# Gated DeltaNet layer: the sample states are updated fifty places later, and two key tiles trade PSUM banks

## The chip, the cores and the metric

The kernel runs on one core of one Trainium2 chip. The metric is the time of one execution on the device, in microseconds (us). TensorE is called PE in the profile, VectorE DVE, ScalarE ACT, GpSimd POOL and SyncE SP.

## The reference, cut to what matters

One inference step of a two-layer trunk on a prompt (16 meta tokens and 1024 tokens) and on eight samples of eight tokens. Layer 0 is a gated DeltaNet with 16 value heads, 8 key heads and a 128x128 state per head; layer 1 is an RWKV-7 mixer. The change is in layer 0:

```
g = -jnp.exp(a_log) * jax.nn.softplus(a + dt_bias)
L = jnp.where(strict, jnp.einsum('nbhik,nbhjk->nbhij', kb, k) * decay, 0.0)
sol = lax.linalg.triangular_solve(L + eye, rhs, lower=True, unit_diagonal=True)
def step(S, inp):                       # per chunk
    v_new = u_c - einsum('bhck,bhkv->bhcv', w_c, S)
    o = einsum('bhck,bhkv->bhcv', qd_c, S) + einsum('bhij,bhjv->bhiv', a_c, v_new)
    S = S * jnp.exp(gl_c)[..., None, None] + einsum('bhck,bhcv->bhkv', kd_c, v_new)
# samples: one chunk of 8 tokens each, S0 = state_gdn; the new S is returned as s_gdn
```

k is L2-normalised, so each key tile needs the squares of its columns before L can be scaled.

## The kernel before

Layer 0 works through eight head pairs j = 0 to 7 (one key head, two value heads h = 0 and 1). The tokens lie in nine tiles of 128: tile 0 holds the 64 sample tokens and the first prompt tokens. Projections run on segments of three tiles (s = 0, 1, 2).

The order on all engines is written out by hand. `Gaps` is a list of places. At each place TensorE gets six matmuls of the running projection (128x384 products), and then everything that was put at that place is issued, sorted by the second number of `put` (a lower one first, ties in the order of the calls). Each engine works its own instructions strictly in that order and waits where an operand is missing. An engine may run ahead of TensorE when its operands allow it, or behind.

Head pair j has its base at place B = 24 + 72 j. Around it:

- `prep_plan` makes the matrix L of pair j. Per segment s: `open_e` loads decays into E, four later steps mask them on GpSimd (L735) and take exponentials on ScalarE; `squares` (L758) multiplies each key tile with itself on TensorE into a PSUM bank and takes the diagonal on VectorE (L766), `rates` (L769 to L773) makes reciprocals, `scaled` (L780) multiplies the bank into E, and `blocks` stores diagonal blocks. The places k of `squares` are B-1, B+4 and B+7 for the three segments; `rates` and the first two tiles of `scaled` follow at k+1, the third tile at k+2. `norms` follows at B+9.
- `invert` inverts the 32x32 diagonal blocks in 31 steps of two instructions (L699, L701) from B+15 to B+48. For pairs 1 to 6 they run on GpSimd, for pairs 0 and 7 on VectorE. At B+49 and B+50 ScalarE copies the transposed inverse (L829), then DMAs spread it, and `merge` joins the blocks from B+57 on.
- `sample_read_plan` loads the sample states of both heads (tiles Sb, three buffers, 256 KB each) at B+12, B+15, B+16 and B+22 and reads them on TensorE at B+20 and B+28.
- `recur_plan` runs the recurrence over the nine tiles from R0 = B + 60, that is 12 places before the next pair's base. Tile t has r0 = R0 + 8 t. At r0: `a` (K times state, TensorE); r0+1: `solve` (X, VectorE L1053); r0+3: `b` (X with the inverse, then w on ScalarE); r0+5: `d` (state update and outputs), `reads`, `tokens`; r0+6: `state` (L1086) and `total` (o, L1107). `a` of the next tile needs the PSUM banks "r" that `total` reads. The sample update `sample_write_plan` is put from here too: per head it loads the state (L963), makes masked copies of tile 0's w on GpSimd (`spread`, L969, four instructions), scales the state on GpSimd (L973, eight instructions), multiplies on TensorE and adds on VectorE (`add`, L982, two banks) and stores (L985). It uses w and ktok of tile 0.
- Weights come in halves: fetch on SP into wraw (two buffers), whi cast on ScalarE, wlo on GpSimd (L150), at places 12 k + 2 and 12 k + 6.
- The convolutions of q, k and v run on ScalarE and VectorE (three taps, L643; tanh; the product L650), the z gate is a tanh on ScalarE and a product on VectorE (L920), one place later.

PSUM tags: "d" (two banks, projections), "r" (two), "f" (two), "m" (one) and "u" (one).

Of the kernel before, what the change touches and what calls it, by code (L numbers as in the profile page):

```python
# [95 lines left out]
class Builder:  # L96
# [8 lines left out]
    def t(self, pool, shape, tag, bufs=1, dt=F32):  # L105
        self.uid += 1
        return pool.tile(shape, dt, name=f"{tag}_{self.uid}", tag=tag, bufs=bufs)
# [638 lines left out]
    def prep_plan(self, j, B, G, o, pace):  # L746

        nc, t, fp, col, L = self.nc, self.t, self.fp, self.col, self.line
        ltd = self.dram([4, 18, 32, 32], f"ltd{j}")
        G.E, c = {}, Ctx()  # L750
        p_ = {}

        def open_e(s):
            G.E[s] = t(fp, [128, 3, 2, 128], "E", 3)
            G.Eg[s] = self.decays(j, s, G.E[s])
            next(G.Eg[s])

        def squares(s):  # L758
            if s == 0:
                c.kq, c.rec, c.bp = t(fp, [128, 9], "kq", 2), t(fp, [128, 9], "rec", 2), t(fp, [128, 9, 2], "bp", 2)  # L760
            p = p_[s] = self.ps(*(("f", 2) if j and s == 2 else ("u", 1)), "sc")
            for tt in range(3):
                b = slice(128 * tt, 128 * tt + 128)
                self.mm(p[:, b], G.K[s][:, b], G.K[s][:, b])
            for tt in range(3):
                nc.vector.scalar_tensor_tensor(p[:, 384:512], p[:, 128 * tt:128 * tt + 128], 1.0, self.ident, op0=ALU.mult, op1=ALU.mult,  # L766
                                               accum_out=c.kq[:, 3 * s + tt:3 * s + tt + 1])

        def rates(s):  # L769
            q3 = slice(3 * s, 3 * s + 3)  # L770
            nc.vector.tensor_scalar(c.kq[:, q3], c.kq[:, q3], 4e-6, None, op0=ALU.add)
            nc.vector.reciprocal(c.rec[:, q3], c.kq[:, q3])
            nc.vector.tensor_tensor(c.bp[:, q3], col[:, q3, 0, 2 * j:2 * j + 2], c.rec[:, q3].unsqueeze(2).broadcast_to([128, 3, 2]),  # L773
                                    op=ALU.mult)

        def scaled(s, *tts):
            E = G.E[s]
            for tt in tts:
                for h in (0, 1):
                    nc.vector.scalar_tensor_tensor(E[:, tt, h], p_[s][:, 128 * tt:128 * tt + 128], c.bp[:, 3 * s + tt, h:h + 1], E[:, tt, h],  # L780
                                                   op0=ALU.mult, op1=ALU.mult)

        def blocks(s):
            E6 = G.E[s].rearrange("p t h k -> p (t h) k")
            for r in range(4):
                b = slice(32 * r, 32 * r + 32)
                nc.sync.dma_start(ltd[r, 6 * s:6 * s + 6].rearrange("c s i -> s c i"), E6[b, :, b])

        G.Eg = {}
        for s in range(3):  # L790
            L.put(B - 10 + 4 * s + o, lambda s=s: open_e(s), 3)
            for u in range(3):
                L.put(B - 6 + 4 * s + o + u, lambda s=s: next(G.Eg[s], None), 2.6)
            L.put(B - 3 + 4 * s + o, lambda s=s: next(G.Eg[s], None), 2.6)
            k = B + (-1, 4, 7)[s] if j else B - 2 + 4 * s + o
            L.put(k, lambda s=s: squares(s), 2)
            L.put(k + 1, lambda s=s: rates(s), 1.8)
            L.put(k + 1, lambda s=s: scaled(s, 0, 1), 2)
            L.put(k + 2, lambda s=s: scaled(s, 2), 2)
            L.put(k + 4, lambda s=s: blocks(s), 3)  # L800
# [84 lines left out]
        for s in range(3):  # L885
            m = merge(s)
# [69 lines left out]
    def sample_write_plan(self, j, G, h, r):  # L956
        nc, t, L = self.nc, self.t, self.line
        hv = 2 * j + h
        Sb, c = {}, Ctx()

        def load(g):
            Sb[g] = t(self.gp, [128, 4, 128], "Sb", 3)
            nc.sync.dma_start(Sb[g], self.i["state_gdn"][0, 4 * g:4 * g + 4, hv].rearrange("b k v -> k b v"))  # L963

        def spread(*bs):
            if bs[0] == 0:
                c.we = t(self.gp, [64, 4, 128], "wexp", 1)
            for b in bs:
                nc.gpsimd.tensor_scalar(c.we[:, b], G.w0[h][0:64], self.bmask4[:, b:b + 1], None, op0=ALU.mult)  # L969

        def scale(g, *us):
            for u in us:
                nc.gpsimd.tensor_scalar(Sb[g][:, u], Sb[g][:, u], self.eglb[:, hv, 4 * g + u:4 * g + u + 1], None, op0=ALU.mult)  # L973

        def add():
            pss = [self.ps("m" if j < 7 else "u", 1, "sw"), self.ps("f", 2, "sw")]
            for g, ps in enumerate(pss):
                q = slice(32 * g, 32 * g + 32)
                self.mm(ps, G.kt0[q, h], c.we[q].rearrange("p b k -> p (b k)"))
            for g, ps in enumerate(pss):  # L980
                x = Sb[g].rearrange("p b k -> p (b k)")
                nc.vector.tensor_tensor(x, x, ps, op=ALU.add)  # L982

        def store(g):
            nc.sync.dma_start(self.o["s_gdn"][0, 4 * g:4 * g + 4, hv].rearrange("b k v -> k b v"), Sb[g])  # L985
        at = (1, 5 if h else 2, 4 if h else 1, 4, 5, 7, 8, 11, 13) if j < 7 else (1, 2, 1, 3, 4, 5, 5, 7, 9)
        for u, f in zip(at, (lambda: load(0), lambda: load(1), lambda: spread(0, 1, 2, 3), lambda: scale(0, 0, 1), lambda: scale(0, 2, 3),
                             lambda: scale(1, 0, 1), lambda: scale(1, 2, 3), add, lambda: (store(0), store(1)))):
            L.put(r + u, f, 2.8)

    def recur_plan(self, j, R0, G, sp):

        nc, t, L, col = self.nc, self.t, self.line, self.col
        hs = (0, 1)
        hv = lambda h: 2 * j + h
        attn, ag, kts, st = {}, {}, {}, {}
# [22 lines left out]
        def tokens(tg):  # L1019
            s, tt = divmod(tg, 3)  # L1020
            p = self.ps("m", 1, "ktok")
            self.transpose(p[:, 0:128], G.K[s][:, 128 * tt:128 * tt + 128])
            kt = kts[tg] = t(self.gp, [128, 2, 128], "ktok", 4)
            for h in hs:
                self.act(kt[:, h], p[:, 0:128], AF.Identity, scale=col[:, tg, 3, hv(h):hv(h) + 1])
            if tg == 0:
                G.kt0 = kt
# [27 lines left out]
        def b(tg):  # L1055
            s, tt = divmod(tg, 3)
            c = st[tg]
            c.w = [t(self.gp, [128, 128], "w", 4) for h in hs]
            if tg == 0:
                G.w0 = c.w  # L1060
            for h in hs:
                self.mm(c.part(h, 1), G.TT[s][:, 2 * tt + h, :], c.X[h])
            if tg:
                for h in hs:
                    self.mm(c.part(h, 3), c.q, G.S[:, h])
            for h in hs:
                self.act(c.w[h], c.part(h, 1), AF.Identity, scale=G.nbp[:, tg, h:h + 1])
# [46 lines left out]

        G.os, G.ssq = {}, {}
        L.put(R0 - 3, lambda: tokens(0), 1.5)
        for tg in range(9):
            r0 = R0 + sp * tg
            for u, f, prio in zip(o_at, (a, solve, b, d, state, reads, total, powers), (1, 1.1, 1, 1, 1.1, 1.2, 1.2, 1.9)):
                L.put(r0 + u, lambda f=f, tg=tg: f(tg), prio)  # L1120
            if tg < 8:
                L.put(r0 + o_at[8], lambda tg=tg: tokens(tg + 1), 1.5)
        for h in hs:
            self.sample_write_plan(j, G, h, R0 + (5 if sp == 8 else 3) + 8 * h)
        for s in range(3):
            n0 = R0 + 3 * sp * (s + 1)
            L.steps(n0, self.gdn_norm(j, G, s), (1, 3, 4, 5, 6), 1.8)
# [1570 lines left out]
```

## Time and profile before

| | us |
|---|---|
| median of three runs | 2204.52 |
| lowest, highest | 2193.73, 2209.86 |
| the profiled execution | 2204.94 |
| its span, first to last instruction | 2203.2 |

One line of the time-ordered view gives the start and the duration of a group of instructions, the engine, the line of the kernel, the operation, the tiles written and read, shapes and count; in square brackets stands how long the engine sat idle before it and whom it waited for. A line of the list of waits gives the total, the number and the longest. A window row gives, per engine, the busy time and the number of instructions, then the granted TensorE clock as a share of full speed.

### The profile page before, as it was taken

What the parts mean: (1) busy time and instruction counts of PE and PEld (TensorE: products, weight loads), DVE (VectorE), ACT (ScalarE), POOL (GpSimd) and SP (SyncE); (2) the same over time, 40 slices, a digit from 0 to 9 for tenths busy, and PEclk for the clock granted to TensorE, in tenths of its full rate; (3) what the DMA queues carried; (4) which work ended last, traced back from release to release, by engine and by line L of the source; (5) the groups of instructions that cost most, each with busy time, mean ns of one, the idle gap of its engine ahead of it and who ended that gap; (6) DMA issues with size and microseconds to landing.
All of it is one profiled execution on the core that took longest, in us unless ns stands there. A gap on an engine that the chain in (4) does not pass through costs nothing.

```text
span 2203.2 us, 56211 instructions
## 1 busy us (share of the span) xinstructions
PE 2087.2 (95%) x20990; PEld 1964.7 (89%) x20990; DVE 1487.7 (68%) x3761; ACT 1246.2 (57%) x3622; POOL 1197.1 (54%) x1788
## 2 busy tenths in 40 slices
PE   8889999999999999988999999999998989999996
PEld 7888989989898989987899999999898988899886
DVE  6867576675757676595533584378875636899976
ACT  5536555655556555654543365575654536777763
POOL 2426758575666858532623163126967424777751
PEclk8999999999999999999999999999999999999998
DMA  3323242424324242433616315478787566776643
GB/s 117 86 74 110 72 115 65 125 78 108 97 74 117 75 110 69 126 84 97 195 58 168 90 55 159 160 233 244 204 241 199 147 183 183 198 195 180 177 133 97
DMA packets 510764, 291.68 MB, mean 132 GB/s; under 512 B 240777, under 2 KB 495866, under 8 KB 510490
## 3 DMA queue, kind: packets, MB, share of 16 engines
q1 hardware_dynamic: 510490, 288.08, 46.7%
q8 instruction: 166, 2.72, 0.5%
q14 instruction: 108, 0.88, 0.1%
HBM read 195.66 MB, written 92.30 MB: 131 GB/s over the span
## 4 chain that ended last, share of the span: by engine, by line
PE 63%; DVE 17%; DMA 7%; ACT 6%; issue 3%; POOL 2%; SPq 2%; DVEq 0%; POOLq 0%; ACTq 0%
PE d L136 14%; PE dv L136 7%; PE dz L136 7%; PE rA L136 6%; PE dk L136 4%; DVE cvy L643 3%; PE rA L140 2%; PE do L136 2%; PE zo L136 2%; DVE E L780 2%; PE xX L140 1%; DMA wraw<-in_gdn_w_out 1%; PE fG L136 1%; DVE invtmp L699 1%; DVE invT L701 1%
## 5 line engine op out<-in xcount | busy, mean ns | idle before, releaser
L150 POOL TENSOR_TENSOR wlo<-wraw,whi 128x512 fp32r<-128x512 f32 x174 | 230.7, 1326 | 250.6 <-ACT whi L146 226.4
L643 DVE SCALAR_TENSOR_TENSOR cvy<-raw,cw,cvy 128x408 f32<-128x408 f32 (+2 forms) x288 | 204.3, 709 | 20.2 <-ACT cvy L122 15.4
L701 POOL TENSOR_TENSOR invT<-invT,invtmp 72x31 f32<-72x31 f32 (+27 forms) x310 | 199.4, 643 | 24.3
L699 POOL TENSOR_TENSOR invtmp<-invA,invT 72x31 f32<-72x31 f32 (+27 forms) x310 | 183.7, 593 | 22.5 <-DMA invA<-rltd 4.5
L136 PE MATMUL d<-xc,whi 128*128 128x384 f32 (+1 forms) x640 | 175.5, 339 | 0.5 <-ACT ev L1455 0.5
L146 ACT CAST whi<-wraw 128x512 fp32r<-128x512 f32 x238 | 146.0, 615 | 33.7 <-DMA wraw<-in_rwkv_w_rkvz 13.2
L136 PE MATMUL dv<-xc,whi 128*128 128x384 f32 (+1 forms) x480 | 156.8, 350 | 0.0
L136 PE MATMUL dz<-xc,whi 128*128 128x384 f32 (+1 forms) x480 | 149.9, 337 | 0.0
L122 ACT ACTIVATE w<-rA,nbp 128x128 f32<-128x128 f32 x144 | 45.3, 364 | 154.1 <-PE rA L136 142.0
L136 PEld LDWEIGHTS d<-xc,whi 128*128 128x128 f32 x640 | 116.8, 190 | 2.6 <-ACT ev L1455 0.9
L136 PE MATMUL d<-xc,wlo 128*128 128x384 f32 (+1 forms) x320 | 104.3, 336 | 1.0 <-DVE wlo L150 1.0
L136 PE MATMUL dv<-xa,whi 128*128 128x384 f32 (+1 forms) x288 | 104.1, 361 | 0.0
L136 PE MATMUL dz<-xa,whi 128*128 128x384 f32 (+1 forms) x288 | 100.3, 348 | 0.8 <-DVE zg L920 0.8
L136 PE MATMUL d<-xa,whi 128*128 128x384 f32 (+1 forms) x336 | 95.4, 336 | 0.7 <-POOL xa L150 0.7
L136 PEld LDWEIGHTS dv<-xc,whi 128*128 128x128 f32 x480 | 94.3, 199 | 0.0
L1967 POOL TENSOR_SCALAR y<-y,mv,grs 128x64 f32<-128x64 f32 x132 | 83.8, 653 | 18.7 <-DVE grs L171 17.1
L167 POOL TENSOR_TENSOR ors<-ovar,cvals 128x6 f32<-128x6 f32 x24 | 34.1, 1421 | 110.0 <-DVE ovar L1136 102.1
L136 PEld LDWEIGHTS dz<-xc,whi 128*128 128x128 f32 x480 | 90.1, 191 | 0.2
L973 POOL TENSOR_SCALAR Sb<-Sb,eglb 128x128 f32<-128x128 f32 x128 | 82.8, 659 | 2.0 <-DVE cvy L643 1.1
L136 PE MATMUL d<-xh,whi 128*128 128x384 f32 (+1 forms) x256 | 82.6, 335 | 0.8 <-ACT xh L146 0.8
L136 PE MATMUL d<-xl,whi 128*128 128x384 f32 (+1 forms) x256 | 82.8, 336 | 0.3 <-DVE sal L1598 0.3
L136 PE MATMUL d<-xh,wlo 128*128 128x384 f32 (+1 forms) x256 | 82.3, 335 | 0.0
(565 smaller groups left out, 7351.3 us busy)
## 6 DMA issues: line engine op xcount, KB each, us to landing
wraw<-in_gdn_w_in SPq DMA_DIRECT2D x96, 256.0 KB
wraw<-in_rwkv_w_rkvz SPq DMA_DIRECT2D x74, 256.0 KB
Sb<-in_state_gdn SPq DMA_DIRECT2D x64, 256.0 KB
wraw<-in_rwkv_w_o SPq DMA_DIRECT2D x48, 256.0 KB
E<-drow SPq DMA_DIRECT2D x24, 384.0 KB
attn<-drow SPq DMA_DIRECT2D x24, 384.0 KB
wraw<-in_gdn_w_out SPq DMA_DIRECT2D x36, 256.0 KB
out_s_gdn<-Sb SPq DMA_DIRECT2D x32, 256.0 KB
```

Source lines behind the costliest of these rows:

```text
L122: return self.nc.scalar.activation(out, in_, func, bias=bias, scale=scale, **kw)
L136: self.nc.tensor.matmul(out, lhsT, rhs, start=start, stop=stop)
L140: self.nc.tensor.matmul(out, lhsT, rhs, start=start, stop=True, skip_group_check=True)
L146: nc.scalar.copy(hi, x)
L150: e.tensor_tensor(lo, x, hi.bitcast(F32), op=ALU.subtract)
L167: self.nc.gpsimd.tensor_tensor(y, x, half.broadcast_to(sh), op=ALU.pow)
L643: nc.vector.scalar_tensor_tensor(ys[s][:, 0:wd(s)], raws[s][:, k:k + wd(s)], cw[k], ys[s][:, 0:wd(s)], op0=ALU.mult, op1=ALU.add)
L699: v.tensor_tensor(tmp, A[:, j, j + 1:32].unsqueeze(2).broadcast_to([nb, n, m]), Tv[:, j, 0:m].unsqueeze(1).broadcast_to([nb, n, m]), op=AL ...
L701: v.tensor_tensor(Tv[:, j + 1:32, 0:m], Tv[:, j + 1:32, 0:m], tmp, op=ALU.subtract)
L780: nc.vector.scalar_tensor_tensor(E[:, tt, h], p_[s][:, 128 * tt:128 * tt + 128], c.bp[:, 3 * s + tt, h:h + 1], E[:, tt, h], op0=ALU.mult, ...
L973: nc.gpsimd.tensor_scalar(Sb[g][:, u], Sb[g][:, u], self.eglb[:, hv, 4 * g + u:4 * g + u + 1], None, op0=ALU.mult)
L1967: nc.gpsimd.tensor_scalar(y[:, q], y[:, q], mv[:, q, 0:1], P.rs[:, q:q + 1], op0=ALU.subtract, op1=ALU.mult)
```

## The change

Three things change, all in layer 0.

1. The sample update of pairs 0 to 6 moves. With P = B + 72, the next pair's base (R0 = P - 12): head 0 had its loads at P-6 and P-5, its mask products at P-6, its scalings at P-3, P-2, P and P+1, its adds at P+4 and its stores at P+6. It now has loads at P+29 and P+30, mask products at P+29, scalings at P+38 to P+41, adds at P+44, stores at P+46. Head 1 had loads at P+2 and P+6, mask products at P+5, scalings at P+5, P+6, P+8 and P+9, adds at P+12, stores at P+14; it now has loads at P+42 and P+47, mask products at P+45, scalings at P+46, P+47, P+49 and P+50, adds at P+52, stores at P+54. Head 0's first bank is "u" in place of "m". Pair 7's update stays where it was.
2. So that w and ktok of tile 0 live that long, they have buffers of their own ("w0" two, "kt0" one); the other tiles' "w" has two buffers in place of four and "ktok" three in place of four.
3. In `prep_plan` of pairs 1 to 7 the second segment's `squares` moves from B+4 to B+1 and into a bank of "f"; the third's, still at B+7, takes "u", in which the first's lies.

```diff
-            p = p_[s] = self.ps(*(("f", 2) if j and s == 2 else ("u", 1)), "sc")
+            p = p_[s] = self.ps(*(("f", 2) if j and s == 1 else ("u", 1)), "sc")
...
-            k = B + (-1, 4, 7)[s] if j else B - 2 + 4 * s + o
+            k = B + (-1, 1, 7)[s] if j else B - 2 + 4 * s + o
...
-            pss = [self.ps("m" if j < 7 else "u", 1, "sw"), self.ps("f", 2, "sw")]
+            pss = [self.ps("m" if h and j < 7 else "u", 1, "sw"), self.ps("f", 2, "sw")]
...
-        at = (1, 5 if h else 2, 4 if h else 1, 4, 5, 7, 8, 11, 13) if j < 7 else (1, 2, 1, 3, 4, 5, 5, 7, 9)
-        for u, f in zip(at, (lambda: load(0), lambda: load(1), lambda: spread(0, 1, 2, 3), lambda: scale(0, 0, 1), lambda: scale(0, 2, 3),
+        if j < 7:
+            r += 51 + 8 * h
+            L.put(r - (7 if h else 15), lambda: spread(0, 1, 2, 3), 2.8)
+            at = (-10, -5, -6, -5, -3, -2, 0, 2) if h else (-15, -14, -6, -5, -4, -3, 0, 2)
+        else:
+            L.put(r + 1, lambda: spread(0, 1, 2, 3), 2.8)
+            at = (1, 2, 3, 4, 5, 5, 7, 9)
+        for u, f in zip(at, (lambda: load(0), lambda: load(1), lambda: scale(0, 0, 1), lambda: scale(0, 2, 3),
                              lambda: scale(1, 0, 1), lambda: scale(1, 2, 3), add, lambda: (store(0), store(1)))):
             L.put(r + u, f, 2.8)
...
-            kt = kts[tg] = t(self.gp, [128, 2, 128], "ktok", 4)
+            kt = kts[tg] = t(self.gp, [128, 2, 128], *(("ktok", 3) if tg else ("kt0", 1)))
...
-            c.w = [t(self.gp, [128, 128], "w", 4) for h in hs]
+            c.w = [t(self.gp, [128, 128], "w" if tg else "w0", 2) for h in hs]
...
-            self.sample_write_plan(j, G, h, R0 + (5 if sp == 8 else 3) + 8 * h)
+            self.sample_write_plan(j, G, h, R0 + 5 if sp == 8 else R0 + 3 + 8 * h)
```

## The prediction, on record before the changed kernel was run

> **What bounds the kernel now.** I read the page first, then the waits of TensorE, then one head pair in the order of time on each engine, then the same stretches as windows.
>
> ```profile
> PE 2087.2 (95%) x20990; PEld 1964.7 (89%) x20990; DVE 1487.7 (68%) x3761; ACT 1246.2 (57%) x3622; POOL 1197.1 (54%) x1788
> PE 63%; DVE 17%; DMA 7%; ACT 6%; issue 3%; POOL 2%; SPq 2%; DVEq 0%; POOLq 0%; ACTq 0%
> PE rA L136 <- DVE o L1107: 24.4, 10, 3.1
> PE mktok L133 <- DVE attn L1011: 6.0, 7, 0.9
> ```
>
> TensorE sets the end, and VectorE holds 17% of the chain that ended last. One wait of TensorE is ten times the rest: a(t), which needs VectorE's total of the tile before. Seven of the ten are one stall that comes once in each head pair. Here it is between pairs 3 and 4. I call P the base place of the following pair, so that a(3) of the old pair is at P+12, b(3) at P+15, b(7) at P+47, d(7) at P+49 and b(8) at P+55.
>
> ```profile
> 563.69 0.60 PE L136 MATMUL rA<-X,TT 128*128 128x128 f32 x4
> ...
> 569.68 0.33 PE L133 MATMUL mktok<-ident,K 128*128 128x128 f32 x1 [0.86 <-DVE attn L1011]
> ...
> 575.56 1.19 PE L136 MATMUL rA<-S,K 128*128 128x128 f32 x4 [2.67 <-DVE o L1107]
> ...
> 584.18 0.61 PE L136 MATMUL rA<-X,TT 128*128 128x128 f32 x4
> ...
> 591.65 0.61 PE L136 MATMUL rA<-S,K 128*128 128x128 f32 x4
> ...
> 592.85 1.08 PE L136 MATMUL usr<-Sb,kqm 128*32 128x128 f32 x32
> ...
> 596.73 0.61 PE L136 MATMUL rA<-X,TT 128*128 128x128 f32 x4
> ```
>
> Three places of work take 8.62 us after the stall (575.56 to 584.18) and 5.08 us one tile later (591.65 to 596.73), though the later stretch holds 32 more matmuls. The windows say why: clock 0.50 after the stall, 1.00 later.
>
> ```profile
> core 0: us, PE busy (x) PEld busy (x) DVE busy (x) ACT busy (x) POOL busy (x), PEclk, DMA share, GB/s
> 575.50:582.00 6.50, 6.44 (x20) 4.64 (x21) 4.24 (x14) 3.24 (x13) 1.02 (x3) 0.50 0.48 132
> 604.40:637.90 33.50, 33.50 (x258) 33.13 (x257) 21.59 (x49) 17.48 (x56) 30.72 (x50) 1.00 0.18 51
> ```
>
> The second row is the stretch to which the change sends work: GpSimd (POOL) is busy 30.72 of 33.50 us there, in 50 instructions with a hand-over between each two.
>
> **The change part by part.** *Removed from P-11 to P+12.* VectorE is behind from 550.7 to 575.6, and these are its rows:
>
> ```profile
> 559.52 0.51 DVE L650 SCALAR_TENSOR_TENSOR K<-raw,cvy 128x336 f32<-128x336 f32 x1 [2.25 <-ACT raw L122]
> ...
> 561.18 0.66 DVE L982 TENSOR_TENSOR Sb<-Sb,msw 128x512 f32<-128x512 f32 x1
> 561.78 0.67 DVE L982 TENSOR_TENSOR Sb<-Sb,fsw 128x512 f32<-128x512 f32 x1
> ...
> 563.29 1.24 DVE L773 TENSOR_TENSOR bp<-gcol,rec 128x6 f32<-128x6 f32 x1
> ...
> 565.61 2.08 DVE L643 SCALAR_TENSOR_TENSOR cvy<-raw,cw,cvy 128x408 f32<-128x408 f32 x2
> ...
> 571.48 0.17 DVE L773 TENSOR_TENSOR bp<-gcol,rec 128x6 f32<-128x6 f32 x1
> ...
> 588.12 1.37 DVE L643 SCALAR_TENSOR_TENSOR cvy<-raw,cw,cvy 128x408 f32<-128x408 f32 x2 [1.02 <-ACT cvy L122]
> ```
>
> The two adds of head 0 go (1.26 us). The bp that took 1.24 beside GpSimd's eight scalings took 0.17 without them (1.07 saved), the two taps 2.08 against 1.37 (0.7). The second tile's norms, now at P+1, fill the 2.25 us in which VectorE waited for ScalarE's tanh; in exchange VectorE waits at P+1 for their six matmuls, which TensorE reaches behind d(1) at about 554.7 and ends 0.85 us later, 1.06 after VectorE is free at 554.49. So 24.9 - 1.26 - 1.07 - 0.7 - 2.25 + 1.06 = 20.7: the total that a(3) needs ends near 571.4. TensorE was there at 575.56 - 2.67 = 572.9; without the 0.86 and without head 0's four matmuls (1.06, next part) it is there at 571.0. The second key tile is ready at 552.3, before its matmuls are reached, so the PSUM bank and the earlier place cost TensorE nothing; without that cover it would wait for the silu. VectorE's total and X of tile 2 come some 0.4 us later than now and may hold a(2) and b(2) by so much. I take a(3) at 571.9, **3.7 us earlier**, with a stall of 0.5 in place of 2.67. The wait of 0.86 has no drop of the clock behind it, so neither should 0.5. Then a(3) to b(3) takes 5.08 less the sample reads (1.08) instead of 8.62: **4.6 us earlier**. In all 8.3, two adds on TensorE (2.1) counted. The same stall in the other pairs:
>
> ```profile
> 199.97 1.09 PE L136 MATMUL rA<-S,K 128*128 128x128 f32 x4 [2.67 <-DVE o L1107]
> ...
> 208.59 0.61 PE L136 MATMUL rA<-X,TT 128*128 128x128 f32 x4
> ...
> 449.65 1.20 PE L136 MATMUL rA<-S,K 128*128 128x128 f32 x4 [2.67 <-DVE o L1107]
> ...
> 459.66 0.60 PE L136 MATMUL rA<-X,TT 128*128 128x128 f32 x4
> ...
> 700.05 0.68 PE L136 MATMUL rA<-S,K 128*128 128x128 f32 x4 [2.67 <-DVE o L1107]
> ...
> 707.05 0.61 PE L136 MATMUL rA<-X,TT 128*128 128x128 f32 x4
> ...
> 947.53 1.12 PE L136 MATMUL rA<-S,K 128*128 128x128 f32 x4 [2.65 <-DVE o L1107]
> ```
>
> From a(3) to b(3) most take 8.6 us; the third takes 10.0 and the fifth 7.0, so their gains are 9.7 and 6.7. Bounds of the gain: 3.0 (only the adds and the two stretched groups, with the rest taken back by the later tanh) and 8.9.
>
> The Trainium skill, "TensorE: Matmul & The Clock Gate", section on HAM oscillation, warns only of idle gaps above some 3.4 us; by it a stall of 2.67 would keep the clock, and the gain would lose 3.5 of its 4.6. No such gap is needed here: 2.67 us were followed by a clock of 0.50, and the measurement decides.
>
> *Added from P+29 to P+54.* Head 0's mask products (P+29), scalings (P+38 to P+41) and adds (P+44), head 1's (P+45, P+46 to P+50, P+52). For pairs 1 to 6 GpSimd works off the triangular inverse there:
>
> ```profile
> 560.64 2.35 POOL L969 TENSOR_SCALAR wexp<-w,bmask 64x128 f32<-64x128 f32 x4 [1.20 <-PE fsw L136]
> 562.97 2.34 POOL L973 TENSOR_SCALAR Sb<-Sb,eglb 128x128 f32<-128x128 f32 x4
> ...
> 604.44 1.27 POOL L150 TENSOR_TENSOR wlo<-wraw,whi 128x512 fp32r<-128x512 f32 x1 [0.44 <-ACT whi L146]
> ...
> 630.70 0.53 POOL L701 TENSOR_TENSOR invT<-invT,invtmp 72x175 f32<-72x175 f32 x1
> ...
> 637.39 0.25 POOL L701 TENSOR_TENSOR invT<-invT,invtmp 72x31 f32<-72x31 f32 x1
> ...
> 642.31 1.30 POOL L150 TENSOR_TENSOR wlo<-wraw,whi 128x512 fp32r<-128x512 f32 x1 [2.89 <-ACT whi L146]
> ...
> 657.00 1.33 POOL L167 TENSOR_TENSOR ors<-ovar,cvals 128x6 f32<-128x6 f32 x1 [11.17 <-DVE ovar L1136]
> ```
>
> From 604.44 to 637.64 it has no idle time; its idle time comes after. Before the inverse's last step stand 4 + 8 + 4 + 4 new instructions: 2.35 + 4.68 + 2.35 + 2.34 = 11.7 us, and the step ends at 649.4 on the old clock. The queues behind it:
>
> ```profile
> 637.67 1.24 ACT L829 COPY invA<-invT 72x256 f32<-72x256 f32 x2
> ...
> 642.13 0.49 ACT L122 ACTIVATE zg<-dz 128x384 f32<-128x384 f32 x1
> ...
> 632.81 0.61 PE L136 MATMUL rA<-X,TT 128*128 128x128 f32 x4
> ...
> 643.89 0.61 PE L136 MATMUL rA<-X,TT 128*128 128x128 f32 x4
> ```
>
> ScalarE's copies of the inverse follow the last step at once (637.64 to 637.67), so there is no slack.
>
> First wait: head 0's second add needs the scalings of P+41, emitted behind the step that ended at 631.23; with 2.35 + 4.68 ahead they end at 638.3. The add stands in VectorE's queue ahead of X of tile 7, so b(7) comes at 638.3 + 0.7 + 0.6 = 639.6 instead of 632.81 + 1.06: TensorE stalls 5.7 us, and its slow clock afterwards runs while GpSimd is still working. Second wait: ScalarE's copies start at 649.4 and the tanh of the z tile, 4.95 us of queue behind them (637.67 to 642.62), ends at 654.4; VectorE's product (0.5) waits for it, head 1's adds stand behind that (1.3), then X (0.6): b(8) at 656.8 instead of 643.89, **12.9 us later**, both adds included. The loads of the inverse move with it and meet merges that are as late; so do the casts. SP's six DMAs per head go to a stretch where it waits for GpSimd anyway; only the fourth load still follows a store by one place. ktok with three buffers and w with two add no wait, since d(t) has read them before b(t+1) writes. Bounds of the loss: 2.1 (all of GpSimd's work hidden, four matmul pairs remain) and 17.
>
> The upper bound is from a stretched row:
>
> ```profile
> 567.28 1.87 POOL L973 TENSOR_SCALAR Sb<-Sb,eglb 128x128 f32<-128x128 f32 x2 [0.22 <-DMA Sb<-in_state_gdn]
> ```
>
> Two scalings took 1.87 beside VectorE's taps, 0.35 more each than 0.59: twelve of the new ones so are 4 us. I take 0.59, since VectorE itself waits from the first add on. The Trainium skill, "SBUF — State Buffer", section on the two sides, has GpSimd blocked for the whole of a VectorE instruction with two SBUF inputs, which the taps are; by it the stretched price holds wherever taps run beside it.
>
> *Sum.* Four pairs 12.9 - 8.3 = +4.6 each, the third +3.2, the fifth +6.2, the last (its inverse is on VectorE, GpSimd has room) 2.1 - 8.3 = -6.2: 18.4 + 3.2 + 6.2 - 6.2 = +22. The profiled execution took 2204.94 us for a span of 2203.2 and lies 0.4 us above the median of the three runs. 2204.94 + 22 = **2227 us**.
>
> **The rivals.** *GpSimd hides it:* 7 x 6.2 = 43 less, 2162 us. For it: 15 us of idle time follow the inverse (2.89 and 11.17 among them). Against it: the copies sit on the inverse without slack. This is the other side of zero, and it decides by whether the last step ends more than some 6 us late. *Only the first wait counts,* as the stretch after b(7) catches up while TensorE's clock is low: loss 5.7 + 2.1 = 7.8, six pairs at -0.5 in the mean and the last at -6.2: 2196 us. *The stretched scalings* of the bound: 6 x 4 more, 2251 us. *The early stall stays:* squares at P+1 push the K taps, tanh and total back, gain 3.0: 6 x 9.9 - 0.9 = +58.5, 2263 us. *The clock would have stayed up without the change too,* in the sense of the page's 3.4 us: gain 3.5 less in seven pairs, 2251 us; the row with 0.50 speaks against it.
>
> **How the numbers follow.** Forecast 0.50, with its own range 2207 to 2247 (2.3 us of loss and 1 of gain in six pairs either way). Hidden 0.18, first wait only 0.15, stretched 0.10, stall stays 0.05, clock 0.02. One per cent is 22 us, about what a measurement of this kernel can tell from no change. Slower by more: 0.25 of the forecast's 0.50 (it lies on that edge) and the last three, 0.42. Within: 0.25 and 0.15, 0.40. Faster: 0.18. The range 2168 to 2256 leaves out the hidden case, up to its near edge, and the stall that stays: 2 in 10 at most.
>
> **What would show it.** The wait of a(3) for o below 1 us in all seven pairs and clock 1.00 behind it; POOL's busy share near full from P+26 to past P+50; ScalarE's copies of the inverse waiting for POOL's last step; VectorE's Sb adds waiting for POOL's scalings; b(7) and b(8) waiting for X, with a slow clock behind b(7). I am wrong if POOL still shows idle time before the last step, or if a(3) still waits.

## The result, and the profile after

| | before | after |
|---|---|---|
| median, us | 2203.11 (six runs, 2193.73 to 2209.86) | 2234.47 (six runs, 2231.77 to 2239.79) |
| span of the profiled execution, us | 2203.2 | 2230.9 |
| mean granted clock | 0.970 | 0.969 |

The ratio is 1.015, 95% interval 1.0122 to 1.0177: **1.5% slower**. In the two spans the difference is 27.7 us, in the medians 31.4 us; what follows accounts for the spans.

First the busy times and the chain that ended last, then lines from the list of waits of the kernel after (total, number of times, longest):

```profile
PE 2092.3 (94%) x20990; PEld 1968.2 (88%) x20990; DVE 1479.1 (66%) x3761; ACT 1245.6 (56%) x3622; POOL 1184.1 (53%) x1788
PE 50%; DVE 14%; POOL 12%; ACT 9%; DMA 8%; issue 4%; SPq 2%; DVEq 0%; POOLq 0%; ACTq 0%
ACT cvy L122 <- POOL raw L628: 38.8, 20, 4.1
ACT invA L829 <- POOL invT L701: 28.5, 6, 4.8
PE rA L136 <- DVE o L1113: 25.1, 16, 3.1
PE msw L136 <- ACT ktok L122: 19.9, 6, 3.3
```

Every engine's busy time is within 1.2% of what it was. But GpSimd, 2% of the chain before, holds 12% of it now, though it is busy 53% of the time. Two of the waits come six times, once in each pair whose inverse runs on GpSimd: ScalarE's copies of the inverse wait for GpSimd's last step, and TensorE's sample matmuls into bank "m" wait for ScalarE's ktok, whose read frees that bank. The wait for o is as long in total as before and sits elsewhere, as TensorE's rows show, from b(3) of pair 2 to b(3) of pair 3:

```profile
456.79 0.68 PE L136 MATMUL rA<-S,K 128*128 128x128 f32 x4 [1.22 <-DVE o L1113]
461.00 0.61 PE L136 MATMUL rA<-X,TT 128*128 128x128 f32 x4
...
496.67 0.68 PE L136 MATMUL rA<-S,K 128*128 128x128 f32 x4 [2.11 <-DVE o L1113]
502.23 0.61 PE L136 MATMUL rA<-X,TT 128*128 128x128 f32 x4
...
516.08 0.75 PE L136 MATMUL rA<-X,TT 128*128 128x128 f32 x4 [1.10 <-DVE X L1059]
...
527.61 0.69 PE L136 MATMUL msw<-wexp,kt 32*128 32x512 f32 x1 [3.31 <-ACT ktok L122]
...
533.48 0.60 PE L136 MATMUL rA<-X,TT 128*128 128x128 f32 x4
...
586.51 0.68 PE L136 MATMUL rA<-S,K 128*128 128x128 f32 x4 [1.22 <-DVE o L1113]
590.73 0.61 PE L136 MATMUL rA<-X,TT 128*128 128x128 f32 x4
```

a(3), a(6), b(7), head 1's matmuls behind a(8), b(8), and the next a(3) and b(3). The stall at a(3) fell from 2.67 to 1.22 us; three new ones stand at a(6), in front of b(7) and in front of b(8). The windows behind a(3), a(6) and head 1's matmuls, and the stretch that the prediction showed at 30.72 of 33.50 us for GpSimd:

```profile
core 0: us, PE busy (x) PEld busy (x) DVE busy (x) ACT busy (x) POOL busy (x), PEclk, DMA share, GB/s
456.80:461.00 4.20, 4.20 (x27) 4.20 (x28) 4.05 (x15) 3.09 (x13) 1.79 (x4) 1.00 0.31 86
496.70:502.20 5.50, 5.50 (x25) 5.50 (x26) 4.12 (x9) 2.27 (x7) 5.19 (x9) 0.69 0.00 0
527.60:533.40 5.80, 5.79 (x22) 4.55 (x23) 2.27 (x5) 4.79 (x15) 4.24 (x6) 0.71 0.55 124
481.00:526.00 45.00, 40.09 (x281) 38.04 (x279) 23.24 (x53) 17.69 (x57) 42.66 (x71) 0.96 0.24 67
```

The low clock has changed places too: 1.00 behind a(3), where it was 0.50, and 0.69 and 0.71 behind two of the new stalls.

Cut at b(3) and b(8), the starts of these matmuls give a balance for every pair (us; the sum of the last two columns is the change of one period):

| pair | b(3) to b(8) before | after | b(8) to next b(3) before | after | loss | gain |
|---|---|---|---|---|---|---|
| first | 60.00 | 72.52 | 64.88 | 57.26 | 12.52 | 7.62 |
| second | 59.87 | 72.50 | 66.32 | 57.25 | 12.63 | 9.07 |
| third | 59.72 | 72.48 | 64.80 | 57.25 | 12.76 | 7.55 |
| fourth | 59.71 | 72.18 | 63.16 | 57.26 | 12.47 | 5.90 |
| fifth | 59.71 | 72.46 | 64.89 | 57.28 | 12.75 | 7.61 |
| sixth | 59.71 | 72.16 | 64.80 | 57.27 | 12.45 | 7.53 |
| last | 86.55 | 91.69 | | | 5.14 | |

The six periods give +30.3 us; the first b(3) comes 7.1 us earlier (201.47 for 208.59), the last pair ends 5.1 later, and 0.6 is won back after it: 27.7.

**How GpSimd's lateness reaches TensorE.** Its own rows, between b(6) and b(8):

```profile
487.83 2.35 POOL L969 TENSOR_SCALAR wexp<-w,bmask 64x128 f32<-64x128 f32 x4
...
492.92 0.18 POOL L628 COPY raw<-raw 128x3 f32<-128x3 f32 x1
...
513.86 1.18 POOL L973 TENSOR_SCALAR Sb<-Sb,eglb 128x128 f32<-128x128 f32 x2
...
525.49 0.25 POOL L701 TENSOR_TENSOR invT<-invT,invtmp 72x31 f32<-72x31 f32 x1
...
546.57 1.36 POOL L167 TENSOR_TENSOR ors<-ovar,cvals 128x6 f32<-128x6 f32 x1 [12.73 <-DVE ovar L1142]
```

and those of ScalarE and VectorE that wait for them:

```profile
493.13 0.62 ACT L122 ACTIVATE cvy<-raw,cw 128x384 f32<-128x384 f32 x1 [4.06 <-POOL raw L628]
...
525.77 1.17 ACT L829 COPY invA<-invT 72x256 f32<-72x256 f32 x2 [4.74 <-POOL invT L701]
526.84 0.63 ACT L122 ACTIVATE ktok<-mktok,gcol 128x128 f32<-128x128 f32 x2
...
493.78 2.03 DVE L643 SCALAR_TENSOR_TENSOR cvy<-raw,cw,cvy 128x384 f32<-128x384 f32 x2 [3.30 <-ACT cvy L122]
...
515.08 0.69 DVE L982 TENSOR_TENSOR Sb<-Sb,fsw 128x512 f32<-128x512 f32 x1 [2.27 <-POOL Sb L973]
...
530.63 0.55 DVE L920 SCALAR_TENSOR_TENSOR zg<-zg,dz 128x384 f32<-128x384 f32 x1 [8.81 <-ACT zg L122]
```

Three chains can be read from them. Head 0's mask products (487.83, 2.35 us) delay a copy of 0.18 us (L628) by which the convolution gets its carried columns; ScalarE's first tap waits 4.06 for it (1.42 before), VectorE's taps 3.30 for ScalarE, o stands behind the taps, and a(6) waits 2.11. The last scaling of head 0 ends at 515.04; the add, X and b(7) follow. The inverse's last step ends at 525.74; the copies start at 525.77, ktok behind them at 526.84, and the sample matmuls at 527.61. And 12.73 us of idle time lie on GpSimd just after all that.

### The profile page after: what moved, and what is told of

The parts are those of the page before. It is cut to its first block, busy times and chain, and to the rows that moved or that the text cites. A ratio compares the mean times of both kernels' runs of the same rounds, so it can differ in the third digit from the quotient of the medians.

```text
span 2230.9 us, 56268 instructions
## 1 busy us (share of the span) xinstructions
PE 2092.3 (94%) x20990; PEld 1968.2 (88%) x20990; DVE 1479.1 (66%) x3761; ACT 1245.6 (56%) x3622; POOL 1184.1 (53%) x1788
## 4 chain that ended last, share of the span: by engine, by line
PE 50%; DVE 14%; POOL 12%; ACT 9%; DMA 8%; issue 4%; SPq 2%; DVEq 0%; POOLq 0%; ACTq 0%
PE d L136 13%; PE dz L136 6%; PE dk L136 4%; PE rA L136 4%; POOL invT L701 3%; POOL invtmp L699 3%; DVE cvy L643 2%; PE do L136 2%; PE rA L140 2%; PE zo L136 2%; POOL wlo L150 2%; POOL Sb L973 2%; PE dv L136 1%; POOL wexp L969 1%; PE xX L140 1%
## 5 line engine op out<-in xcount | busy, mean ns | idle before, releaser
L643 DVE SCALAR_TENSOR_TENSOR cvy<-raw,cw,cvy 128x408 f32<-128x408 f32 (+2 forms) x288 | 198.2, 688 | 40.0 <-ACT cvy L122 35.0
L136 PE MATMUL dz<-xc,whi 128*128 128x384 f32 (+1 forms) x480 | 157.8, 355 | 0.0
L136 PE MATMUL dv<-xc,whi 128*128 128x384 f32 (+1 forms) x480 | 150.7, 337 | 0.0
L136 PE MATMUL dz<-xa,whi 128*128 128x384 f32 (+1 forms) x288 | 107.1, 372 | 0.8 <-DVE zg L920 0.8
L136 PEld LDWEIGHTS dz<-xc,whi 128*128 128x128 f32 x480 | 97.2, 205 | 0.2
L136 PEld LDWEIGHTS dv<-xc,whi 128*128 128x128 f32 x480 | 89.7, 190 | 0.0
L150 DVE TENSOR_TENSOR wlo<-wraw,whi 128x512 fp32r<-128x512 f32 x64 | 49.5, 774 | 52.1 <-ACT whi L146 40.6
```

The source lines that it names most:

```text
L136: self.nc.tensor.matmul(out, lhsT, rhs, start=start, stop=stop)
L150: e.tensor_tensor(lo, x, hi.bitcast(F32), op=ALU.subtract)
L643: nc.vector.scalar_tensor_tensor(ys[s][:, 0:wd(s)], raws[s][:, k:k + wd(s)], cw[k], ys[s][:, 0:wd(s)], op0=ALU.mult, op1=ALU.add)
```

## The experiments

All are compared with the kernel before, on the same chip and in the same rounds; its median was 2197.14 us in the rounds of the first four and 2205.37 in those of the last four.

**1. The norms alone.** The kernel before with only the third part of the change:

```diff
-            p = p_[s] = self.ps(*(("f", 2) if j and s == 2 else ("u", 1)), "sc")
+            p = p_[s] = self.ps(*(("f", 2) if j and s == 1 else ("u", 1)), "sc")
...
-            k = B + (-1, 4, 7)[s] if j else B - 2 + 4 * s + o
+            k = B + (-1, 1, 7)[s] if j else B - 2 + 4 * s + o
```

> The kernel before with the third part of the change alone: the second segment's squares at P+1 in a bank of f, the third's in u. Theory (GpSimd has no room at P+29 to P+50, and that costs 12.8 us a pair against an early gain of 8): this part does no harm; VectorE's wait of 2.25 us at P+4 goes, 1.1 us of waiting at P+1 comes, so a(3) waits 1 to 2 us and 2172 to 2198 us come out. Rival (the norms' new place and bank cause the loss, by holding up the taps of K): 2210 us or more, with a(2) or a(3) waiting longer than before.

Measured: 2182.35 us, ratio **0.9923** (0.9894 to 0.9952). The wait of a(3) is short here although no sample update has moved, and a new wait, seven times 1.44 us, stands in front of head 0's second sample bank:

```profile
550.29 1.12 PE L136 MATMUL fsw<-wexp,ktok 32*128 32x512 f32 x2 [1.44 <-DVE E L780]
...
563.58 0.68 PE L136 MATMUL rA<-S,K 128*128 128x128 f32 x4 [0.85 <-DVE o L1107]
...
569.05 0.61 PE L136 MATMUL rA<-X,TT 128*128 128x128 f32 x4
```

From a(3) to b(3) it takes 5.47 us for 8.62 before, head 1's sample matmuls included in both; b(3) to b(8) stays at 59.7 in four of the six pairs and is 60.6 in the other two. The stall of a(3) is short because TensorE comes late, held up by the new wait: from b(8) to a(3) it takes 56.9 us in the mean of six pairs, for 56.2 before. What is won here lies behind a(3), where the clock is 1.00 in the window from 563.6 to 569.0. So a part of the change that is a gain was bound together with one that costs more.

**2. The move alone.** The kernel after, with those two lines put back.

> The changed kernel with the norms back at their old place and bank: the sample update moved, alone. Theory: GpSimd's queue is as in the changed kernel, so the stalls at a(6), b(7) and msw stay: 2225 to 2245 us. Rival (the norms cause the loss): 2160 to 2195 us, without these stalls.

Measured: 2248.1 us, ratio **1.0225** (1.0159 to 1.029), a little above the expected range. b(3) to b(8) takes 71.64 us, nearly as long as in the full change, and a(3) still waits:

```profile
PE rA L136 <- DVE o L1113: 37.5, 16, 3.2
PE msw L136 <- ACT ktok L122: 13.2, 6, 3.3
...
453.88 0.68 PE L136 MATMUL rA<-S,K 128*128 128x128 f32 x4 [2.92 <-DVE o L1113]
...
583.98 0.68 PE L136 MATMUL rA<-S,K 128*128 128x128 f32 x4 [2.93 <-DVE o L1113]
```

Taking two adds and eight scalings out of the early stretch does not shorten the stall. It does bring a(3) forward: from b(8) to a(3) it takes 54.2 us in the mean of six pairs, for 56.2 before. TensorE is there sooner too, 51.3 us behind b(8) in place of 53.6, so the stall, which is the difference of the two, hides what VectorE has gained. And a(3) to b(3) takes 4.22 us in five of the seven pairs in spite of the stall. From b(8) to b(3) the move alone wins 5.9 us a pair of the 7.6 that the full change wins. VectorE still waits for the tanh in front of the product of K; with the norms moved as well, in the kernel after, it does not:

```profile
439.91 0.51 DVE L650 SCALAR_TENSOR_TENSOR K<-raw,cvy 128x336 f32<-128x336 f32 x1 [1.97 <-ACT raw L122]
...
446.27 0.51 DVE L650 SCALAR_TENSOR_TENSOR K<-raw,cvy 128x336 f32<-128x336 f32 x1
```

The first row is from this experiment, the second from the kernel after.

**3. The added work on ScalarE.** The kernel after, with the mask products and scalings of pairs 0 to 6 at the same places on ScalarE:

```diff
+                if j < 7:
+                    self.act(c.we[:, b], G.w0[h][0:64], AF.Identity, scale=self.bmask4[:, b:b + 1])
+                    continue
...
+                if j < 7:
+                    self.act(Sb[g][:, u], Sb[g][:, u], AF.Identity, scale=self.eglb[:, hv, 4 * g + u:4 * g + u + 1])
+                    continue
```

> The changed kernel, with the mask products and scalings of pairs 0 to 6 on ScalarE in place of GpSimd, at the same places. Theory: GpSimd's queue is 14 us a pair shorter, ScalarE's copies of the inverse wait no longer, 9 us a pair more on ScalarE (24 x 0.37) fit beside its 17.5 of 33.5 us; the loss falls from 12.8 to between 2 and 5 us a pair: 2160 to 2190 us. Rival (the late adds themselves, their banks, or the smaller buffers of w and ktok cost the time, whatever engine scales): 2225 us or more.

Measured: 2191.45 us, ratio **0.9956** (0.9928 to 0.9983), just above the expected range. b(3) to b(8) falls from 72.48 to 65.08 us, the stall at a(6) and the one for ktok are gone, and b(8) waits for X:

```profile
511.67 0.64 PE L136 MATMUL rA<-X,TT 128*128 128x128 f32 x3 [2.73 <-DVE X L1065]
```

**4. The added work left out.** The kernel after, with one mask product in place of four and no scalings in pairs 0 to 6:

```diff
+            if j < 7:
+                nc.gpsimd.tensor_scalar(c.we, G.w0[h][0:64].unsqueeze(1).broadcast_to([64, 4, 128]), self.bmask4[:, 0:1], None, op0=ALU.mult)
+                return
...
-            for u in us:
+            for u in us if j == 7 else ():
```

> The changed kernel without the scalings of the sample state in pairs 0 to 6, and with one mask product of 64x512 in place of four: this part of the computation is left out, loads, adds and stores stay. GpSimd has 2.6 us a pair in place of 14. Theory: the stalls at a(6), b(7) and msw go almost wholly, 2155 to 2180 us. Rival (adds, banks or buffers): 2225 us or more.

Measured: 2192.0 us, ratio **0.9955** (0.9932 to 0.9978); slower than expected. b(3) to b(8) still takes 64.55 us, 4.8 more than before, and b(8) waits 1.48 us:

```profile
504.07 0.56 DVE L920 SCALAR_TENSOR_TENSOR zg<-zg,dz 128x384 f32<-128x384 f32 x1 [6.28 <-ACT zg L122]
504.54 0.68 DVE L985 TENSOR_TENSOR Sb<-Sb,msw 128x512 f32<-128x512 f32 x1
...
506.14 0.75 PE L136 MATMUL rA<-X,TT 128*128 128x128 f32 x4 [1.48 <-DVE X L1062]
```

So of the 12.76 us that this pair loses in the full change, 7.9 go with GpSimd's added work and 4.8 stay: 2.1 for four matmul pairs, 1.48 for this stall, 0.46 for a short one at a(6), and 0.8 of small changes. (The new buffers of w and ktok were not tested by themselves; what they cost is within these 4.8.) Head 1's adds stand in VectorE's queue between the gate's product, which waits for ScalarE anyway, and X. On top of the norms the move wins 5.1 us between b(8) and b(3) (62.4 in experiment 1 in the mean of six, 57.3 after) and loses these 4.8: even with GpSimd's work for nothing it would be worth about nothing. What also makes the whole slower than expected is the last pair, whose stretch from b(3) to b(8) takes 96.2 us here, for 86.6 before.

**5. GpSimd's time alone.** The kernel before, its sample update where it was, and 24 useless GpSimd instructions per pair at the places to which the change sends work:

```diff
+        if j < 7:
+            def more(n):
+                d = t(self.gp, [128, 104], "more", 1)
+                for _ in range(n):
+                    nc.gpsimd.tensor_scalar(d, self.ident[:, 0:104], self.eglb[:, hv, 0:1], None, op0=ALU.mult)
+            P = r + (7 if h == 0 else -1)
+            for u, n in ((45, 4), (46, 2), (47, 2), (49, 2), (50, 2)) if h else ((29, 4), (38, 2), (39, 2), (40, 2), (41, 2)):
+                L.put(P + u, lambda n=n: more(n), 2.8)
```

> The kernel before, sample update untouched, with 24 useless GpSimd instructions of 128x104 in pairs 0 to 6, at the places to which the change moves the mask products and scalings. They write a tile that nobody reads. Theory (GpSimd has no room there): the inverse's last step comes some 9 us later, ScalarE's copies of it wait 4 us or more, a(6) waits 2 us, and the time rises by 5 to 9 us in six pairs: 2225 to 2255 us. Rival (what costs time is VectorE's late adds, which wait for the scalings and hold up X; GpSimd alone is hidden): within 8 us of the kernel before.

Measured: 2279.22 us, ratio **1.0342** (1.0309 to 1.0375), more than expected:

```profile
ACT invA L829 <- POOL invT L701: 48.8, 6, 9.2
PE rA L136 <- DVE X L1061: 46.3, 10, 7.6
ACT cvy L122 <- POOL raw L628: 36.7, 13, 4.2
...
516.21 0.68 PE L136 MATMUL rA<-S,K 128*128 128x128 f32 x4 [2.21 <-DVE o L1115]
...
551.25 1.22 PE L136 MATMUL rA<-X,TT 128*128 128x128 f32 x4 [6.89 <-DVE X L1061]
```

The same waits come back without one DMA, matmul or add being moved: a(6) behind the copy of L628, the copies of the inverse behind the last step. b(3) to b(8) takes 70.81 us, 11.1 more than before, and b(8) to b(3) 2.1 more (66.9 for 64.8 in the mean of six): 13.2 in each of six pairs are 79, and the spans differ by 73.3 (2276.5 and 2203.2). That GpSimd's lateness alone slows the kernel is shown. The 11.1 us are more than the 7.9 that went in experiment 4, since the two costs of the change do not add up: GpSimd's work alone costs 11.1 (here), the rest alone 4.8 (experiment 4), both together 12.6. That fits two paths to b(8) of which the later sets its start.

**6. What the early stall hangs on.** The kernel before, its update where it was, with the mask products cut to one and the scalings left out as in experiment 4.

> The kernel before without the scalings of the sample state in pairs 0 to 6 and with one mask product in place of four (this part of the computation is left out); adds and norms stay where they were. Theory (GpSimd's scalings stretch VectorE's instructions with two SBUF inputs from P to P+9, by 1.8 us a pair): bp takes 0.17 and the two taps 1.4 us, a(3) waits about 1 us in place of 2.67, and with a clock that then stays up 2165 to 2185 us come out. Rival (these rows were long for another reason): a(3) still waits over 2.3 us, 2195 to 2205 us.

Measured: 2200.35 us, ratio **0.9988** (0.9967 to 1.0009): no difference. VectorE's taps do get shorter, and a(3) waits as long as ever:

```profile
556.30 0.97 DVE L773 TENSOR_TENSOR bp<-gcol,rec 128x6 f32<-128x6 f32 x1
...
558.34 1.31 DVE L643 SCALAR_TENSOR_TENSOR cvy<-raw,cw,cvy 128x408 f32<-128x408 f32 x2
...
567.82 1.19 PE L136 MATMUL rA<-S,K 128*128 128x128 f32 x4 [2.94 <-DVE o L1110]
```

The taps took 2.08 us before and take 1.31; bp took 1.24 and still takes 0.97; and further on nbp (L805), 0.21 before, takes 1.01. b(8) to b(3) is 0.5 us shorter in the mean of six pairs (64.27 for 64.81), b(8) to a(3) 0.8 (55.5 for 56.2). Of the 1.77 us that the prediction put down to these two groups, less than half was there to be won.

**7. The norms, with the new wait mended.** Experiment 1, and head 0's second sample bank from "u", since "f" now holds the second segment's squares at that time:

```diff
-            pss = [self.ps("m" if j < 7 else "u", 1, "sw"), self.ps("f", 2, "sw")]
+            pss = [self.ps("m" if j < 7 else "u", 1, "sw"), self.ps(*(("f", 2) if h or j == 7 else ("u", 1)), "sw")]
```

> The norms alone, and head 0's second add bank is u in place of f (pairs 0 to 6). With the norms alone msw's partner fsw waited 1.44 us in each of seven pairs for scaled(1), which holds an f bank at P+4. Theory: that wait goes, what TensorE does next comes as much earlier unless VectorE is late: 2168 to 2180 us against 2182 for the norms alone. Rival (VectorE is the bound there and a(3) waits longer instead): 2180 to 2185 us, with a(3)'s wait grown by about 1.4 us.

Measured: 2172.71 us, ratio **0.9862** (0.983 to 0.9893), with experiment 8 the fastest version found, ahead of both kernels. The wait for E is gone; part of it comes back at a(3), which TensorE now reaches sooner. From b(8) to a(3) it takes 54.8 us in the mean of six pairs, for 56.2 before, so here the norms do bring a(3) forward:

```profile
562.78 0.68 PE L136 MATMUL rA<-S,K 128*128 128x128 f32 x4 [1.57 <-DVE o L1107]
...
568.26 0.61 PE L136 MATMUL rA<-X,TT 128*128 128x128 f32 x4
```

**8. The same, with mask products and scalings on ScalarE** (the edit of experiment 3 on top of 7).

> As the run with the norms and the bank u, and the mask products and scalings of pairs 0 to 6 on ScalarE at their early places. Theory (GpSimd's share of the early stretch slows VectorE, and ScalarE has room): a(3)'s wait goes wholly, 2160 to 2178 us. Rival (ScalarE is full from P-3 to P+9: exponentials, casts, tanh): tanh and w come later, 2185 us or more.

Measured: 2174.39 us, ratio **0.9864** (0.9825 to 0.9903), the same as 7. Where the update stands early, the engine that scales doesn't matter, which agrees with experiment 6. The wait of a(3), expected to go wholly, stays at 1.53 us. Putting the added work into GpSimd's 12.73 idle us was not tried.

## Why the prediction was right, point by point

**The balance** was forecast as 8.3 gained and 12.9 lost in a pair, +4.6; measured are 7.6 and 12.6, +5.0. The two odd pairs came out as read from their old stalls: +3.56 for the forecast +3.2, +6.57 for +6.2. In the whole: a first gain of 7.1 for 8.3, six periods of +30.3 for +27.8, the last pair +5.1 for +2.1, in all 27.7 for 22.

**The loss** was right where it was worked out from GpSimd's queue. Counted from b(3), head 0's scalings were to end at 638.3 - 584.18 = 54.1 us and ended at 515.04 - 461.00 = 54.0; the inverse's last step at 65.2 for a measured 64.7; b(8) at 72.6 for 72.5. In the six pairs the added instructions took 0.59 us each (1.18 for two, 2.35 for four), not the stretched 0.94, so that rival is out; VectorE has no taps beside the scalings there. The unstretched price, and that no cover was left ahead of the last step, carried the forecast; experiment 5 shows that GpSimd's time suffices as a cause, experiments 3 and 4 that without it on that engine 7.4 and 7.9 us of the loss go. That b(8) came out to 0.1 us is in part luck: it went by another path of nearly the same length, as the second point below says.

**Where it was wrong on the way:**
- The 5.7 us that b(7) was to wait are 1.10. b(7) is 6.4 us later than before, for 6.8 forecast, but TensorE had lost 3.9 of it at a(6), by the chain through the copy of L628 that the prediction didn't have, and by a clock of 0.69 behind it (a(6) to b(6) 5.56 us for 3.89).
- The second wait was put on X, behind the gate's product and head 1's adds. TensorE met ktok and bank "m" first. The forecast path runs almost level: X starts at 532.29, takes 0.60, and b(8) starts at 533.48.
- a(3) waits 1.22 us, not 0.5, and the clock stayed at 1.00 behind it as forecast: 0.7 us of the gain. So two of the named signs failed: the wait was to be below 1 us and is 1.20 to 1.25 in all seven pairs, and the slow clock was to stand behind b(7), where it is 1.00; it stands behind a(6) and head 1's matmuls.
- The last pair lost 5.1 us, not 2.1. Its stretch from b(3) to b(8) has a mean clock of 0.89 for 0.96. It is GpSimd's added work that can be ruled out: with that on ScalarE or left out (experiments 3 and 4), the stretch takes 97.3 and 96.2 us, more than the 91.7 after. Without the move (experiments 1 and 7) it takes 85.2 and 85.3. So the loss comes with the rest of the move; which wait causes it was not tested.
- TensorE's wait for o was three times the next in its list, not ten times (24.4 us; 7.7 for a DMA and 6.0 for attn). Nothing in the sum rests on this.

**The early gain** came out in both halves: counted from the b(8) before it, a(3) came 3.2 us earlier for 3.7 forecast, and a(3) to b(3) took 4.4 us less for 4.6. Means of the six pairs that follow another, in us:

| | b(8) to TensorE at a(3) | stall | b(8) to a(3) | a(3) to b(3) |
|---|---|---|---|---|
| before | 53.6 | 2.7 | 56.2 | 8.6 |
| experiment 6, scalings out | 52.5 | 3.0 | 55.5 | 8.8 |
| experiment 1, norms | 56.3 | 0.6 | 56.9 | 5.5 |
| experiment 7, norms and bank | 53.2 | 1.6 | 54.8 | 6.0 |
| experiment 2, move | 51.3 | 2.9 | 54.2 | 4.7 |
| after, move and norms | 51.8 | 1.2 | 53.0 | 4.2 |

In all of them a(3) starts when o is ready, so the third column times VectorE. The move brings o 2.1 us forward, of which the scalings are worth 0.8 (experiment 6) and the adds, by difference, 1.3, for 1.26 in the sum; these rows stand behind the wait for the tanh, VectorE's last ahead of this o. The norms bring 1.1 more on top of it, for the sum's 2.25 - 1.06 = 1.19. The term that was mis-sized is the stretched groups, 0.8 for 1.77: where some rows get shorter, others get longer, as nbp does, with 1.01 us in experiment 6 and 0.99 in experiment 2 for 0.21 before. The stall by itself would mislead here, for it also depends on when TensorE comes: it is longest where only the scalings are out, and shortest in experiment 1, where o is latest.

The second half came out, but its reason is not shown. The forecast had the clock stay up because the stall gets short; in experiment 2 the stall is as long as ever, and behind five of the seven a(3) to b(3) takes 4.22 us all the same, with a clock of 1.00. So this half is luck in part, and what keeps the clock up stays open.

**The rivals.** *GpSimd hides it* is out by the copies of L829, which waited 4.7 us. *Only the first wait* is out by the stall ahead of b(8). *The early stall stays:* in the full change it falls to 1.22 us; it stays in the move without the norms, but there the gain is 5.9 us a pair and not the 3.0 of that rival. *The clock would have stayed up without the change:* out, since the seven stalls before were each followed by 7.0 to 10.0 us from a(3) to b(3), for 4.2 after, of which head 1's matmuls are some 1.3 (5.48 in experiment 1, 4.22 after).

## What to carry to other kernels

Before work is moved to an engine "with room", look at that engine's idle time in the stretch where it will stand, and at what is queued behind it there: GpSimd was idle 46% of the span and 12.7 us at one go just afterwards, and still the added instructions delayed a copy of 0.18 us and an inverse on which three other engines waited. When a change has two parts, price and run them apart; here one part was worth 0.8% by itself, 1.4% with a bank changed, and was buried under the other. And do not judge a saving by the length of a stall. A stall is the difference of two arrivals: here the late engine gained 2.1 us and the stall grew, because the waiting engine came 2.3 us sooner. Time from one fixed point, as from b(8) to a(3), shows what was won.

## What the runs showed of the hardware that was not expected

A stall of one length does not always have one consequence for the granted clock. Windows behind three stalls at a(3), a(3) and a(6) in the kernel of experiment 2, of 2.92, 2.93 and 2.10 us:

```profile
453.90:458.10 4.20, 4.20 (x28) 4.20 (x28) 4.05 (x15) 3.08 (x13) 1.81 (x4) 1.00 0.55 137
584.00:589.70 5.70, 5.70 (x27) 5.70 (x28) 4.43 (x17) 3.08 (x13) 3.30 (x7) 0.70 0.56 156
493.80:497.70 3.90, 3.90 (x25) 3.90 (x26) 2.56 (x8) 1.81 (x7) 3.59 (x7) 1.00 0.00 0
```

2.92 was followed by 1.00 and 2.93 by 0.70; 2.10 by 1.00, where 2.11 in the kernel after was followed by 0.69. And one of 1.71 us, at the first a(3) of experiment 7, was followed by 0.54, with 1.00 behind 1.57 a few pairs later:

```profile
200.00:207.40 7.40, 7.40 (x24) 6.10 (x23) 4.69 (x14) 1.98 (x8) 3.87 (x9) 0.54 0.69 186
443.00:448.30 5.30, 5.30 (x31) 4.38 (x32) 4.80 (x15) 2.95 (x13) 2.15 (x3) 1.00 0.70 182
```

That one event is 3.1 us (a(3) to b(3) 8.60 there, 5.48 in four pairs); the last two pairs of that experiment take 7.02 and 7.04, behind stalls of 1.57 and 1.56, with a clock of 0.76. In the kernel before, all seven stalls of 2.64 to 2.67 us were followed by 7.0 to 10.0 us from a(3) to b(3). The Trainium skill, "TensorE: Matmul & The Clock Gate", section on HAM oscillation, warns of gaps above some 3.4 us; the traces disagree, with falls behind gaps of 1.56 to 2.93 us. So a length from which the clock falls can't be read from these runs. The prediction's step, that 0.5 us would keep the clock up as 0.86 did, rested on one kind of gap, though it came out: no stall of a(3) of 1.25 us or less was followed by a fall in any of these runs, and one of 1.57 was and was not. What else decides is open.
